# A two-layer hybrid encoder on one core: 32x32 products in half bursts, later diagonal copies, early products in a fixed order

## The chip, the cores and the metric

The kernel runs on one core of a Trainium2 chip. The metric is the device time of one execution in microseconds (us); less is better. The core has a matrix engine (TensorE, PE in the profile, its weight loads PEld), a vector engine (VectorE, DVE), a scalar engine (ScalarE, ACT), GpSimd (POOL) and a sync engine (SyncE, SP) that issues most of the transfers. Each engine runs its own instructions in the order in which they were placed on it, and waits for the others where data or room require it.

## The reference

The reference is an encoder of two layers over 1040 tokens (16 learned ones ahead of 1024) of width 1024, all in 32-bit floating point. Each layer normalises its input, multiplies it by one input matrix, and splits the result. One part feeds a gated delta rule in both directions, 4 heads of 128; the other part is a short gated convolution. Both are joined, multiplied by an output matrix and added to the input. A gated feed-forward block (gate and up, width 2816, then down) follows.

What matters here is the triangular system of the delta rule:

```python
M = jnp.where(strict, jnp.einsum('bnhid,bnhjd->bnhij', kb, k) * decay_mat, 0.0)
A = M + jnp.eye(CHUNK, dtype=M.dtype)
u = lax.linalg.triangular_solve(A, vb, left_side=True, lower=True, unit_diagonal=True)
...
def step(S, inp):
    u_c, w_c, qd_c, kd_c, a_c, gl_c = inp
    v_new = u_c - jnp.einsum('bhcd,bhde->bhce', w_c, S)
    o = jnp.einsum('bhcd,bhde->bhce', qd_c, S) + jnp.einsum('bhij,bhje->bhie', a_c, v_new)
    S = S * gl_c[..., None, None] + jnp.einsum('bhcd,bhce->bhde', kd_c, v_new)
    return S, o
```

The kernel takes chunks of 128 tokens instead of 64, and inverts the 128x128 triangles of all 8 full chunks and 4 heads (32 of them) at once, for each of the two directions.

## The kernel before, in words

**Precision and products.** A 32-bit product is made of three on TensorE: every weight and every input is split into a rounded part (`hi`, copied by ScalarE, line 126) and the rest (`lo`, subtracted by VectorE, line 127), and the matmuls are hi x hi, hi x lo, lo x hi (lines 153, 154, 155). A dense chunk is one call of the inner loop of `dense`: 24 matmuls over 256 to 512 tokens into one bank. Weights come by SyncE's transfers in tiles of 128x512 (`raw`, two buffers), and three buffers each hold their `whi` and `wlo`.

**The order of the work.** A planner places every instruction: it takes the ready instruction of smallest priority number on each engine, by times that it simulates itself, and the engines then run in that order. The code sets priorities: after the first half of a layer the dense matmuls get late ones (`mmp`), so that they fill what other work leaves; `low(f)` places a small product in the same row as the dense ones. Behind each dense chunk `dense` takes one job from each of three lists (`jobs`, `jobs2`, `jobs3`), so that a list of jobs becomes one job a chunk. `after(ins, prev)` adds an edge: `ins` is placed behind `prev`. `wsplit` (line 120) leaves its ScalarE copy in `whi_done[0]`.

**The inverse.** `chunk_p` writes the triangles to `Pv[0]` and `Pv[1]`, one for each direction. `sub_start` (line 524) copies the 32x32 blocks on the diagonal with four ScalarE copies a direction (line 535) and turns them with one VectorE transpose (line 537); the copies of the first direction go to `v[3]`, those of the second to `v[1]` of a scratch tile. `substitute(d)` then inverts all 32x32 blocks by 31 steps of two VectorE instructions (lines 547 and 549). `invert(d)` (line 551) puts the blocks together. It returns jobs: `first` makes 64 products of 32x32 (line 574) and copies them; `second_third` makes 96 (lines 587 and 588), 48 into one bank and 48 into another, each bank with its ScalarE copies (lines 592 and 593) and VectorE copies (lines 594 to 596); five calls of `fourth_fifth` make the 64x64 products (lines 607 and 609). So there are 7 jobs a direction, in `jobs3`: those of the first direction from the last of the four value tiles (line 752), those of the second from the fourth of the eight z and convolution tiles.

**The scan.** `scan_step` (line 815) runs the recurrence chunk by chunk, both directions beside each other. Its scratch `rec` takes the place of the inverse's scratch. The last step of the second direction is the last reader of `Pv[1]` (line 853), whose place the split outputs `oh` and `ol` take (lines 974 and 975). Dense products of the convolution and output projection fill TensorE under the scan.

**The early products.** The feed-forward block uses a scheme with seven half-size products in place of eight. For the first four rows f of the gate and up matrices, the two products of one of its seven (q = 0 and q = 1) are made early, in `early_part(f, q)` (line 1087), beside the end of the output projection: a weight tile is loaded and split (lines 1043 and 1044), then `prod` (line 1056) makes 12 matmuls (lines 1061 to 1063) for each of `NJ` column groups (two of 260 tokens in the first layer, one of 512 in the second), and ScalarE copies the sum out (line 1097). q = 1 adds to the bank that q = 0 filled and that line 1097 has just read. T tiles are prepared meanwhile by `t_split` (lines 1010 and 1011).

Of the kernel before, what the change touches and what calls it, by code (L numbers as in the profile page):

```python
# [42 lines left out]
def trunk(ctx: ExitStack, tc: tile.TileContext, xT, w_in, w_ba, w_out, w_gu, w_dn,  # L43
# [21 lines left out]
    def c4k(tag="c"):  # L65
        return sb.tile([128, L], F32, tag="c", bufs=2, name=nm(tag))
# [47 lines left out]
    mmp = [None]  # L114
    evp = [None]
    jobs, jobs2, jobs3 = [], [], []
    whi_done = [None]
    lov = [False]

    def wsplit(src, hi, lo, raw=None):  # L120

        kk = src.shape[1]
        if raw is None:
            raw = wp.tile([128, WK, 128], F32, tag="raw", bufs=2, name=nm("raw"))
        dma(raw[:, 0:kk, :], src)
        whi_done[0] = act(out=hi, in_=raw[:, 0:kk, :], func=AF.Copy)  # L126
        tt(out=lo, in0=raw[:, 0:kk, :], in1=hi.bitcast(F32), op=ALU.subtract)  # L127

    def wload(src, nk):

# [165 lines left out]
    for l in range(DEPTH):  # L296
# [224 lines left out]
        subs = {}  # L521
        Tm = None

        def sub_start():

            nonlocal Tm
            tmp0.append(big(Y[0][2]))
            Tm = sb.tile([128, 2, 128], F32, tag="off", name=nm("Tm")).rearrange("p a b -> p (a b)")
            v = [tmp0[0][:, i, 0:1024] for i in range(4)]
            for d in range(2):  # L530
                W, Xi = (v[0], v[2]) if d == 0 else [c4k("x")[:, 0:1024] for _ in range(2)]
                W, Xi, dg = (t.rearrange("p (a b) -> p a b", a=32) for t in (W, Xi, v[3 - 2 * d]))
                dma(Xi, eye_d)
                for b in range(4):
                    act(out=dg[B[b]], in_=Pv[d][B[b], :, B[b]], func=AF.Copy)

                nc.vector.transpose(out=W, in_=dg.rearrange("p q i -> p i q"))
                subs[d] = W, Xi

        def substitute(d):  # L540
            W, Xi = subs[d]
# [9 lines left out]
        def invert(d):  # L551
# [15 lines left out]
            def fb(c):  # L567
                return bank("fb"[d]).rearrange("p (q c) -> p q c", c=c)
# [7 lines left out]
                    for (f, s) in pairs:  # L576
                        act(out=QS[B[s], qs, :], in_=ps[B[s]], func=AF.Copy, scale=-1.0)

            def second_third():
                f0, s0 = pairs[0]  # L580
                fo, so = 32 * (f0 % 2), 32 * (s0 % 2)
                for qs in halves:
                    ps = fb(32)

                    def turn(q):
                        for (f, s) in pairs:
                            mm(ps[B[f], q - qs.start, :], QS[B[s], q, :], P_[B[s], q, B[s]], start=True, stop=True, skip_group_check=True)
                        mm(ps[B[s0], q - qs.start, :], P_[B[s0], q, B[s0]], QS[B[s0], q, :], start=True, stop=True, skip_group_check=True)

                    low(lambda: [turn(q) for q in range(qs.start, qs.stop)])  # L590
                    for (f, s) in pairs:
                        act(out=P_[B[f], qs, B[s]], in_=ps[B[f]], func=AF.Copy)
                    act(out=X64[B[s0], qs, fo:fo + 32], in_=ps[B[s0]], func=AF.Copy)
                    nc.vector.tensor_copy(X64[B[f0], qs, fo:fo + 32], XB[B[f0], qs, :])
                    nc.vector.tensor_copy(X64[B[s0], qs, so:so + 32], XB[B[s0], qs, :])
                    nc.vector.memset(X64[B[f0], qs, so:so + 32], 0.0)


            F_, S_ = (slice(0, 64), slice(64, 128)) if d == 0 else (slice(64, 128), slice(0, 64))
# [1 line left out]
            def fourth_fifth(q4, q5):  # L601

                ps = fb(64)

                def turn(q):
                    if q4 is not None:
                        mm(ps[S_, q, :], P_[F_, 8 * q4 + q, S_], X64[F_, 8 * q4 + q, :], start=True, stop=True, skip_group_check=True)
                    if q5 is not None:
                        mm(ps[F_, q, :], X64[S_, 8 * q5 + q, :], P_[S_, 8 * q5 + q, S_], start=True, stop=True, skip_group_check=True)
# [443 lines left out]
        CW = E if E * 4 > 1024 else NB  # L1053
        NJ = NB // CW

        def prod(ps, w, t, j, first, stop=True):
            nk = w[0].shape[1]
            for k in range(nk):
                cs = slice(CW * j, CW * j + CW)
                th, tl = (t[0][k], t[1][k]) if isinstance(t[0], list) else (t[0][:, k, :], t[1][:, k, :])  # L1060
                mm(ps[:, :CW], w[0][:, k, :], th[:, cs], start=first and k == 0, stop=False, skip_group_check=True)  # L1061
                mm(ps[:, :CW], w[0][:, k, :], tl[:, cs], start=False, stop=False, skip_group_check=True)  # L1062
                mm(ps[:, :CW], w[1][:, k, :], th[:, cs], start=False, stop=stop and k == nk - 1, skip_group_check=True)  # L1063

        def raw4(tag):
            if tag == "raw":
# [16 lines left out]

        NE = 4
        early, bks0 = {}, {}

        def early_part(f, q):

            A = raw4("raw")
            dma(A, w_gu[l, f, 0, :, 4 * q:4 * q + 4, :])  # L1090
            w = w_op(A, True)
            if q == 0:
                early[f] = (row(Y[1], F32, 3), row(X[1], F32, 3)) if f < 3 else (row(Y[1] + "f"), c4k())
                bks0[f] = [pbank() for j in range(NJ)]
            for j in range(NJ):
                prod(bks0[f][j], w, T[("B11", "B21")[q]], j, q == 0)
                act(out=part(early[f][1 - q], 0, j), in_=pin(bks0[f][j]), func=AF.Copy)  # L1097

        npar = sb.tile([128, 4], F32, tag="npar", name=nm("npar"))
# [525 lines left out]
```

## Time and profile before

| what | value |
|---|---|
| time, median of 3 runs | 2476.99 us |
| lowest and highest | 2471.99 and 2478.96 us |
| time of the profiled execution | 2479.11 us |
| span of the profiled execution, first to last instruction | 2477.3 us |
| mean granted TensorE clock in it | 0.996 |
| VectorE busy | 1778.2 us, 72% of the span |
| ScalarE busy | 1054.9 us, 43% of the span |

The span is shorter than the time by 1.8 us that lie around it. The profile is one execution, so a sum worked out from its rows stands beside 2479.11 us, not beside the median. Rows of the timeline give start, duration, engine, line, operation, the tile written and the tiles read, size, count, and in brackets how long the engine had been idle and what ended that. Rows by stretches give the busy time of each engine, the granted clock (PEclk; 1.00 is full) and the share of the DMA engines. "issue" as a releaser means that nothing the profile shows ended the wait.

### The profile page before, as it was taken

What the parts mean: (1) busy time and instruction counts of PE and PEld (TensorE: products, weight loads), DVE (VectorE), ACT (ScalarE), POOL (GpSimd) and SP (SyncE); (2) the same over time, 40 slices, a digit from 0 to 9 for tenths busy, and PEclk for the clock granted to TensorE, in tenths of its full rate; (3) what the DMA queues carried; (4) which work ended last, traced back from release to release, by engine and by line L of the source; (5) the groups of instructions that cost most, each with busy time, mean ns of one, the idle gap of its engine ahead of it and who ended that gap; (6) DMA issues with size and microseconds to landing.
All of it is one profiled execution on the core that took longest, in us unless ns stands there. A gap on an engine that the chain in (4) does not pass through costs nothing.

```text
span 2477.3 us, 44868 instructions
## 1 busy us (share of the span) xinstructions
PE 2450.6 (99%) x17530; PEld 2255.6 (91%) x17530; DVE 1778.2 (72%) x3296; ACT 1054.9 (43%) x1964; POOL 67.3 (3%) x157
## 2 busy tenths in 40 slices
PE   9999999999999999999999999999999999999998
PEld 8989999999999999999999888998978888888887
DVE  6888355769877777877657884456798777678774
ACT  6654333445333333444446543334553333334544
POOL 0120000000000000000001100000000000000002
PEclk9999999999999999999999999999999999999999
DMA  4545353534223332674224443445442233238641
GB/s 133 160 146 190 114 166 118 192 93 141 101 94 108 110 102 79 208 238 150 89 83 155 146 159 116 149 138 200 124 139 90 97 107 113 94 106 259 198 138 69
DMA packets 201321, 335.26 MB, mean 135 GB/s; under 512 B 23404, under 2 KB 88356, under 8 KB 201108
## 3 DMA queue, kind: packets, MB, share of 16 engines
q1 hardware_dynamic: 172996, 293.83, 36.9%
q10 hardware_dynamic: 25936, 34.19, 4.3%
q0 software_dynamic: 2176, 4.36, 0.6%
q8 instruction: 138, 2.26, 0.4%
q14 instruction: 75, 0.61, 0.1%
HBM read 250.31 MB, written 81.99 MB: 134 GB/s over the span
## 4 chain that ended last, share of the span: by engine, by line
PE 90%; DVE 4%; DMA 3%; ACT 2%; issue 1%; SPq 0%; ACTq 0%; DVEq 0%
PE pacc L155 10%; PE pacc L153 10%; PE pacc L154 10%; PE pacc L1063 4%; PE pacc L1061 4%; PE pacc L1062 4%; PE pb L1063 3%; PE pb L1061 3%; PE pb L1062 3%; PE pf L1063 3%; PE pf L1061 3%; PE pf L1062 3%; PE pacc L1484 2%; PE pacc L1481 2%; PE pacc L1483 2%; PE pa L1061 1%
## 5 line engine op out<-in xcount | busy, mean ns | idle before, releaser
L153 PE MATMUL pacc<-a,whi 128*128 128x346 f32 (+1 forms) x800 | 262.3, 328 | 1.5 <-ACT whi L126 1.0
L155 PE MATMUL pacc<-a,wlo 128*128 128x346 f32 (+1 forms) x800 | 261.1, 327 | 1.3 <-DVE wlo L127 1.2
L153 PE MATMUL pacc<-b,whi 128*128 128x346 f32 (+2 forms) x672 | 234.5, 349 | 0.6 <-ACT whi L126 0.6
L155 PE MATMUL pacc<-b,wlo 128*128 128x346 f32 (+2 forms) x672 | 233.7, 349 | 0.8 <-DVE wlo L127 0.8
L154 PE MATMUL pacc<-a,whi 128*128 128x346 f32 (+1 forms) x681 | 222.9, 328 | 1.3 <-DVE a L174 0.6
L154 PE MATMUL pacc<-b,whi 128*128 128x346 f32 (+2 forms) x580 | 200.8, 346 | 0.0
L126 ACT ACTIVATE whi<-raw 128x512 fp32r<-128x512 f32 x166 | 104.3, 631 | 218.3 <-PE pacc L154 158.2
L127 DVE TENSOR_TENSOR wlo<-raw,whi 128x512 fp32r<-128x512 f32 x166 | 113.6, 686 | 66.2 <-ACT whi L126 62.6
L155 PEld LDWEIGHTS pacc<-a,wlo 128*128 128x128 f32 x800 | 151.3, 189 | 4.0 <-DVE wlo L127 1.8
L153 PEld LDWEIGHTS pacc<-a,whi 128*128 128x128 f32 x800 | 151.2, 189 | 3.9 <-ACT whi L126 1.2
L153 PEld LDWEIGHTS pacc<-b,whi 128*128 128x128 f32 x672 | 127.2, 189 | 12.2 <-issue 1.9
L155 PEld LDWEIGHTS pacc<-b,wlo 128*128 128x128 f32 x672 | 126.9, 189 | 10.7 <-issue 1.3
L154 PEld LDWEIGHTS pacc<-a,whi 128*128 128x128 f32 x681 | 128.8, 189 | 5.0 <-DVE a L174 1.3
L1043 ACT ACTIVATE whi<-rw 128x512 fp32r<-128x512 f32 x92 | 57.9, 633 | 142.4 <-PE pf L1062 40.8
L154 PEld LDWEIGHTS pacc<-b,whi 128*128 128x128 f32 x580 | 109.8, 189 | 7.0 <-issue 0.4
L1043 ACT ACTIVATE b<-rw 128x512 fp32r<-128x512 f32 x64 | 40.1, 631 | 134.3 <-PE pacc L1062 42.1
L1043 ACT ACTIVATE a<-rw 128x512 fp32r<-128x512 f32 x64 | 40.3, 631 | 93.0 <-PE pacc L1062 60.0
L313 DVE TENSOR_TENSOR a<-pacc,rstd 128x346 f32<-128x346 f32 (+2 forms) x59 | 32.6, 554 | 59.7 <-PE pacc L155 59.4
L1044 DVE TENSOR_TENSOR wlo<-rw,whi 128x512 fp32r<-128x512 f32 x92 | 62.6, 684 | 3.4 <-ACT whi L1043 3.1
L313 DVE TENSOR_TENSOR b<-pacc,rstd 128x346 f32<-128x346 f32 (+1 forms) x63 | 32.2, 513 | 45.2 <-PE pacc L155 45.2
L1061 PE MATMUL pacc<-b,whi 128*128 128x260 f32 (+1 forms) x172 | 53.3, 310 | 0.2 <-ACT c L1097 0.2
L1062 PE MATMUL pacc<-b,whi 128*128 128x260 f32 (+1 forms) x172 | 53.3, 310 | 0.0
(981 smaller groups left out, 7863.6 us busy)
## 6 DMA issues: line engine op xcount, KB each, us to landing
raw<-in_w_in SPq DMA_DIRECT2D x110, 256.0 KB
raw<-in_w_gu SPq DMA_DIRECT2D x104, 256.0 KB
rw<-in_w_gu SPq DMA_DIRECT2D x88, 256.0 KB
rw<-in_w_dn SPq DMA_DIRECT2D x94, 192.0 KB
rec<-vkd SPq DMA_DIRECT2D x61, 256.0 KB
raw<-in_w_out SPq DMA_DIRECT2D x48, 256.0 KB
b<-ad SPq DMA_DIRECT2D x45, 260.0 KB
a<-ad SPq DMA_DIRECT2D x45, 256.0 KB
```

The source lines that it names most:

```text
L126: whi_done[0] = act(out=hi, in_=raw[:, 0:kk, :], func=AF.Copy)
L127: tt(out=lo, in0=raw[:, 0:kk, :], in1=hi.bitcast(F32), op=ALU.subtract)
L153: mm(ps[:, :n], wh, xh[:, n0:n1], start=(k == 0), stop=False)
L154: mm(ps[:, :n], wh, xl[:, n0:n1], start=False, stop=False)
L155: mm(ps[:, :n], wl, xh[:, n0:n1], start=False, stop=(k == K - 1))
L313: tt(out=t[:, n0:n1], in0=ps, in1=rstd[:, n0:n1], op=ALU.mult)
L1043: act(out=hi, in_=src, func=AF.Copy)
L1044: tt(out=lo, in0=src, in1=hi.bitcast(F32), op=ALU.subtract)
L1061: mm(ps[:, :CW], w[0][:, k, :], th[:, cs], start=first and k == 0, stop=False, skip_group_check=True)
L1062: mm(ps[:, :CW], w[0][:, k, :], tl[:, cs], start=False, stop=False, skip_group_check=True)
L1063: mm(ps[:, :CW], w[1][:, k, :], th[:, cs], start=False, stop=stop and k == nk - 1, skip_group_check=True)
L1481: one = mm(ps[:, :CW], wh[:, k, :], th[:, cs], start=st, stop=False, skip_group_check=True)
```

## The change

There are three parts.

1. `second_third` takes one half (16 of the 32 triangles) as its argument and is given to `jobs3` twice. So there are 8 jobs a direction instead of 7, and 48 products of 32x32 follow each other instead of 96.
2. `sub_start` takes the direction. It runs for the first direction at once as before. For the second direction its four copies and its transpose become jobs of `jobs3`, at the 4th, 5th, 7th, 8th and 9th chunk of the value tiles. Each copy is placed behind the weight copy that was issued last (`whi_done[0]`), the transpose behind the last `lo` subtraction (`whi_done[1]`, new).
3. The first matmul of each product of `early_part` is placed behind the last matmul of the product before it, over both column groups, both q and all four f.

```diff
-        whi_done[0] = act(out=hi, in_=raw[:, 0:kk, :], func=AF.Copy)
-        tt(out=lo, in0=raw[:, 0:kk, :], in1=hi.bitcast(F32), op=ALU.subtract)
...
+        whi_done[1] = tt(out=lo, in0=raw[:, 0:kk, :], in1=hi.bitcast(F32), op=ALU.subtract)
...
-            for d in range(2):
-                W, Xi = (v[0], v[2]) if d == 0 else [c4k("x")[:, 0:1024] for _ in range(2)]
...
-                dma(Xi, eye_d)
-                for b in range(4):
-                    act(out=dg[B[b]], in_=Pv[d][B[b], :, B[b]], func=AF.Copy)
-
-                nc.vector.transpose(out=W, in_=dg.rearrange("p q i -> p i q"))
-                subs[d] = W, Xi
+            dma(Xi, eye_d)
+            subs[d] = W, Xi
+            steps = [lambda b=b: after(act(out=dg[B[b]], in_=Pv[d][B[b], :, B[b]], func=AF.Copy), whi_done[0] if d else None) for b in range(4)]
+            return steps + [lambda: after(nc.vector.transpose(out=W, in_=dg.rearrange("p q i -> p i q")), whi_done[1] if d else None)]
...
-            def second_third():
+            def second_third(qs):
...
-                for qs in halves:
-                    ps = fb(32)
...
+                ps = fb(32)
...
-            return [first, second_third] + [lambda a=a, b=b: fourth_fifth(a, b) for a, b in ((0, None), (1, 0), (2, 1), (3, 2), (None, 3))]
+            return [first] + [lambda qs=qs: second_third(qs) for qs in halves] + [lambda a=a, b=b: fourth_fifth(a, b) for a, b in ((0, None), (1, 0), (2, 1), (3, 2), (None, 3))]
...
-        sub_start()
+        for f in sub_start(0):
+            f()
...
+        st1 = sub_start(1)
+        jobs3.extend([None, None, None, st1[0], st1[1], None, st1[2], st1[3], st1[4]])
...
-        def prod(ps, w, t, j, first, stop=True):
+        def prod(ps, w, t, j, first, stop=True, prev=None):
...
-                mm(ps[:, :CW], w[0][:, k, :], th[:, cs], start=first and k == 0, stop=False, skip_group_check=True)
+                one = mm(ps[:, :CW], w[0][:, k, :], th[:, cs], start=first and k == 0, stop=False, skip_group_check=True)
+                if prev is not None and k == 0:
+                    after(one, prev)
...
+                one = mm(ps[:, :CW], w[1][:, k, :], th[:, cs], start=False, stop=stop and k == nk - 1, skip_group_check=True)
+            return one
...
+        turn_e = [None]
...
-                prod(bks0[f][j], w, T[("B11", "B21")[q]], j, q == 0)
+                turn_e[0] = prod(bks0[f][j], w, T[("B11", "B21")[q]], j, q == 0, prev=turn_e[0])
```

More of the change, by code (lines that the diff above doesn't have):

```diff
@@ L116, in trunk @@
     jobs, jobs2, jobs3 = [], [], []
-    whi_done = [None]
+    whi_done = [None, None]
     lov = [False]
@@ L577, in first, with turn @@
                         act(out=QS[B[s], qs, :], in_=ps[B[s]], func=AF.Copy, scale=-1.0)
-            def second_third():
+            def second_third(qs):
                 f0, s0 = pairs[0]
                 fo, so = 32 * (f0 % 2), 32 * (s0 % 2)
-                for qs in halves:
-                    ps = fb(32)
[L585 to L590, printed above, removed]
-                    for (f, s) in pairs:
[L592 to L596, printed above, removed]
+                ps = fb(32)
+                def turn(q):
+                    for (f, s) in pairs:
+                        mm(ps[B[f], q - qs.start, :], QS[B[s], q, :], P_[B[s], q, B[s]], start=True, stop=True, skip_group_check=True)
+                    mm(ps[B[s0], q - qs.start, :], P_[B[s0], q, B[s0]], QS[B[s0], q, :], start=True, stop=True, skip_group_check=True)
+                low(lambda: [turn(q) for q in range(qs.start, qs.stop)])
+                for (f, s) in pairs:
+                    act(out=P_[B[f], qs, B[s]], in_=ps[B[f]], func=AF.Copy)
+                act(out=X64[B[s0], qs, fo:fo + 32], in_=ps[B[s0]], func=AF.Copy)
+                nc.vector.tensor_copy(X64[B[f0], qs, fo:fo + 32], XB[B[f0], qs, :])
+                nc.vector.tensor_copy(X64[B[s0], qs, so:so + 32], XB[B[s0], qs, :])
+                nc.vector.memset(X64[B[f0], qs, so:so + 32], 0.0)
             F_, S_ = (slice(0, 64), slice(64, 128)) if d == 0 else (slice(64, 128), slice(0, 64))
```

11 lines of the change are left out of this document (6 added, 5 removed).

## The prediction

> **What bounds the kernel now.** I read the page first, then the waits of TensorE, then the timeline around the longest of them, then the stretches for the clock.
>
> ```profile
> span 2477.3 us, 44868 instructions
> ...
> PE 2450.6 (99%) x17530; PEld 2255.6 (91%) x17530; DVE 1778.2 (72%) x3296; ACT 1054.9 (43%) x1964; POOL 67.3 (3%) x157
> ...
> q8 instruction: 138, 2.26, 0.4%
> ```
>
> TensorE is the bound: its 99% leaves 27 us in which it does nothing. No part of the change removes a product, so it can only win from such gaps and from time at a lower clock. The waits of TensorE, longest in total first (engine, what waited, what for: us, times, longest):
>
> ```profile
> PE pf L587 <- issue: 2.5, 2, 2.1
> PE pb L1061 <- ACT whi L1043: 2.0, 1, 2.0
> ...
> PE pb L587 <- issue: 1.9, 1, 1.9
> ```
>
> Line 587 belongs to `second_third` and 1061 to the early products; the waits for weight splits, part 2, are of the same size and follow with their rows.
>
> **Part 1, half bursts.** One call of `second_third` appears in the rows of its two lines, then the burst in the second layer's first and second direction and in the first layer's first direction:
>
> ```profile
> L587 PE MATMUL pf<-P,a x128: 191/191/256, 1448.6 to 1452.9; 32*32 32x32 f32 x128
> ...
> L588 PE MATMUL pf<-a,P x64: 191/191/256, 1448.6 to 1452.9; 32*32 32x32 f32 x64
> ```
> ```profile
> 1450.46 0.19 PE L588 MATMUL pf<-a,P 32*32 32x32 f32 x1
> 1452.72 0.26 PE L587 MATMUL pf<-P,a 32*32 32x32 f32 x2 [2.07 <-issue]
> ...
> 1523.09 0.21 PE L587 MATMUL pb<-P,a 32*32 32x32 f32 x2 [1.89 <-issue]
> ...
> 208.37 0.22 PE L587 MATMUL pf<-P,b 32*32 32x32 f32 x2 [0.40 <-issue]
> ```
>
> A call is 128 + 64 = 192 matmul records and as many weight loads, 384 instructions. From 1448.6 to 1450.46 they pass at about 5 ns each (12 records of the 192 come after the stall), then TensorE stands with nothing to wait for. The page's instruction queue says what is missing: 2.26 MB over 2 x 17530 instructions is 64 bytes each, and 2.26 MB over 138 packets is 16.4 KB, or some 256 instructions a packet. Narrowed to 1450.2 to 1451.2, the view of the queues shows one such packet, and none from 1443.5 to 1450.2:
>
> ```profile
> q8 instruction: 1, 0.02, 5.5%
> ```
>
> TensorE goes on about 2.5 us after that packet starts, so the instructions ran out. Over the whole span an instruction takes 2477 / 35060 = 71 ns, so 256 last 18 us. In the burst they last 256 x 5 ns = 1.3 us. A half has 192 instructions and takes 1 us; a chunk of 48 lies between the halves, and it takes about 4 us (a chunk and one later job take 5.08 us in the rows of the scan term). So any 256 last 1 + 4 = 5 us, twice the 2.5 us. I take the stalls as gone: 2.07 + 1.89 + 0.40 us idle, and 0.19 us each for the last product ahead of it, under which the next ones would have started, **4.9 us**. The fourth call, at 272.8, has no such row, so a stall depends on where the packets' borders fall. `first` stays as it is, and has no such wait in its four calls.
>
> Each long stall was followed by a stretch at half clock (its row: length, busy time of PE, PEld, DVE, ACT and POOL, granted clock, DMA share, GB/s):
>
> ```profile
> 1452.74:1456.15 3.41, 3.41 (x22) 2.86 (x23) 1.85 (x5) 2.36 (x4) 0.00 (x0) 0.50 0.02 5
> 1524.42:1527.83 3.41, 3.41 (x9) 2.63 (x8) 0.00 (x0) 0.88 (x2) 0.00 (x0) 0.50 0.00 0
> 1821.38:1824.79 3.41, 3.41 (x9) 2.62 (x9) 3.41 (x6) 1.46 (x3) 0.00 (x0) 0.50 0.27 76
> ...
> 152.26:155.67 3.41, 2.02 (x11) 1.73 (x12) 3.36 (x5) 2.21 (x4) 3.14 (x7) 1.00 0.14 37
> ```
>
> TensorE is busy throughout, so 3.41 us at 0.50 lose 1.7 us. Two of the three belong to the bursts: **3.4 us**. (The last row shows that 1.4 us idle in such a stretch did not bring the next one down.) Part 1: 8.3 us.
>
> The Trainium skill, "Runtime: NRT & Kernel Launch", section "Instruction fetch mechanics", gives TensorE room for 2048 instructions, refilled in blocks of 256. By that rule a burst of 384 would not run dry, part 1 would bring nothing, and the time would be that of the third rival below; the packet that lands inside the stall speaks against it.
>
> **Part 2, diagonal copies.** ScalarE, VectorE and TensorE in the first layer, then the second layer:
>
> ```profile
> L535 ACT ACTIVATE b<-P x8: 1041/1056/1062, 143.2 to 150.7; 32x1024 f32<-32x1024 f32 x8
> ...
> 151.79 1.15 ACT L126 ACTIVATE whi<-raw 128x512 fp32r<-128x512 f32 x2
> ...
> 169.42 0.63 ACT L126 ACTIVATE whi<-raw 128x512 fp32r<-128x512 f32 x1 [1.58 <-PE pacc L154]
> ```
> ```profile
> 147.50 2.08 DVE L537 STREAM_TRANSPOSE b<-b 128x1024 f32<-128x1024 f32 x1 [2.18 <-ACT b L535]
> ```
> ```profile
> 152.47 0.42 PE L153 MATMUL pacc<-a,whi 128*128 128x348 f32 x1 [0.99 <-ACT whi L126]
> ...
> 154.87 0.42 PE L155 MATMUL pacc<-a,wlo 128*128 128x348 f32 x1 [1.19 <-DVE wlo L127]
> ...
> 1393.27 0.43 PE L153 MATMUL pacc<-b,whi 128*128 128x348 f32 x1 [0.65 <-ACT whi L126]
> ...
> 1395.70 0.43 PE L155 MATMUL pacc<-b,wlo 128*128 128x348 f32 x1 [0.77 <-DVE wlo L127]
> ```
>
> The weight copies for the first value tile stand behind eight diagonal copies on ScalarE. With four of them gone they start 4 x 1.06 = 4.2 us earlier, at 147.5, and end at 148.7, ahead of TensorE's need at 151.5. The `lo` parts are late next: VectorE is free of the first transpose at 149.6 and gives them at 150.3 and 150.9, still in time. So all four waits go: 0.99 + 1.19 + 0.65 + 0.77 = 3.6 us, and 0.1 us more for each matmul that starts cold (0.42 for 0.32): **4.0 us**. Left over would be at most the `lo` waits, 2.0 us.
>
> The four copies (4.3 us) and the transpose (2.0 us) come back later, behind weight copies of the second and third value tile. What queues behind them on ScalarE is the silu and convolution of the value tiles and the next weight copy. That one waits for TensorE to free its buffer (1.58 us idle at 169.42, with a whole tile of three chunks, 12 us, still to run before it is needed), so they cost nothing; without that cover two copies in a row would cost 2.1 us each time. The transposed blocks are needed by the second substitution, whose first instruction runs at 198.3:
>
> ```profile
> L547 DVE TENSOR_TENSOR Tm<-x,x x62: 180/360/425, 198.3 to 1487.1; 128x31 f32<-128x31 f32 x4, 128x60 f32<-128x60 f32 x4, 128x87 f32<-128x87 f32 x4, 128x112 f32<-128x112 f32 x4
> ```
>
> Even the ninth chunk ends ahead of that (152.5 + 9 x 4 = 188.5). The scratch `v[1]` is written again only in the second half of `second_third`, some 20 us later. The transfer of the unit blocks is issued on SyncE's queue a little later, for the same use.
>
> **Part 3, early products.** TensorE and ScalarE in the first layer's and second layer's early products:
>
> ```profile
> 588.72 0.39 PE L1061 MATMUL pf<-b,whi 128*128 128x260 f32 x1 [0.45 <-ACT whi L1043]
> ...
> 592.79 0.39 PE L1063 MATMUL pf<-b,wlo 128*128 128x260 f32 x1 [0.68 <-DVE wlo L1044]
> ...
> 603.23 0.39 PE L1061 MATMUL pa<-a,whi 128*128 128x260 f32 x1 [0.77 <-ACT c L1097]
> ```
> ```profile
> 1818.23 0.39 PE L1063 MATMUL pacc<-a,wlo 128*128 128x512 f32 x1
> 1820.65 0.50 PE L1061 MATMUL pb<-a,whi 128*128 128x512 f32 x1 [2.03 <-ACT whi L1043]
> ...
> 1821.21 0.52 PE L1061 MATMUL pacc<-b,whi 128*128 128x512 f32 x1
> ```
> ```profile
> 1820.50 0.58 ACT L1097 ACTIVATE b<-pacc 128x512 f32<-128x512 f32 x1
> ```
>
> At 1820.65 two matmuls of row f = 2 (bank `pb`) stand ahead of f = 1, q = 1 (`pacc<-b`), and wait for their weights. In order, `pacc<-b` would be first. But it adds to a bank that line 1097 reads until 1821.08, so it could not start before 1821.2 in any order: the wait stays, and the two matmuls that were done meanwhile come later (0.5 us). In the first layer two column groups hide that read, and the order saves perhaps what it costs. Where the next `lo` parts are late, VectorE is full (3.41 of 3.41 us in the third half-clock row), and the order does not speed it up. Bounds: all four waits and one half-clock stretch go, -5.6 us; or the two first matmuls of each product lose their cover, 7 borders x 0.47 in the second layer and 15 x 0.24 in the first, +6.9 us. I take **0**, by the last row, and count the edge itself (same engine, same order) as free.
>
> **What the extra job costs.** The second direction's last job comes one chunk later, and the scan starts behind it. Two of these jobs, then the scan's last step of the second layer (its last input on ScalarE, its products on TensorE):
>
> ```profile
> 1547.77 0.27 PE L607 MATMUL pb<-a,P 64*64 64x64 f32 x1
> ...
> 1552.85 1.14 PE L609 MATMUL pb<-P,a 64*64 64x64 f32 x16
> ...
> 1760.88 1.05 PE L853 MATMUL pb<-vv,P 128*128 128x128 f32 x8
> ...
> 1762.24 0.28 PE L153 MATMUL pacc<-o,whi 128*128 128x256 f32 x1
> ```
> ```profile
> 1755.29 1.15 ACT L850 ACTIVATE qs<-pb,negE 128x128 f32<-128x128 f32 x4 [1.16 <-PE pb L848]
> ```
>
> So the scan starts 5.08 us later against the dense work. Its last products run at 1760.88, though their last input was there at 1756.44: 4.44 us of slack. The output products, which need the room that those products free, begin at once behind them. 5.08 - 4.44 leaves **0.6 us**; nothing at best, 5.1 us if the planner keeps its distances. In the first layer the last output is split at 521.6 and first used at 532.9, so 5.08 us there cost nothing:
>
> ```profile
> 520.13 1.44 DVE L975 TENSOR_TENSOR o<-b,o 128x260 fp32r<-128x260 f32 x4
> ```
> ```profile
> 532.89 0.28 PE L153 MATMUL pf<-o,whi 128*128 128x260 f32 x1
> ```
>
> **Sum.** 2479.1 - 8.3 - 4.0 + 0 + 0.6 = 2467.4 us, from the profiled execution; that one lies 2.1 us above the median of the runs shown, so the gain against the median is 9.6 us, 0.39%. A measurement of this kernel tells about 0.3%, 7.4 us, from no change: 2469.6 is the border.
>
> **Rivals.** (a) The order also wins the waits of part 3: 2467.4 - 5.6 = 2461.8 us. For it: four such rows; against: the read of the bank at 1820.50. (b) The scan's delay is all seen: 2467.4 + 4.5 = 2471.9 us. For it: output products right behind line 853; against: 4.44 us of slack. (c) The stall belongs to these products, whatever the burst's length, so part 1 does nothing: 2479.1 - 4.0 + 0.6 = 2475.7 us. Against it: the call at 272.8 without a stall. (d) Slower: the fixed order takes TensorE's cover at each of the second layer's 7 borders between early products, and each shows the gap of 1818.23 to 1821.21 (2.6 us beyond a matmul), with three more half-clock stretches: 7 x 2.6 - 2.0 + 3 x 1.7 = 21.3, so 2488.7 us. It decides the sign from (11.7 + 2.0) / 7 = 2.0 us a border. For it: line 1097 must be passed every second border, and the planner filled those gaps with later products; against: at the other borders no bank is shared.
>
> **Chances.** Forecast 0.55 (2463 to 2472 by itself, about three quarters of that below 2469.6: 0.41 faster, 0.14 same); (a) 0.10, faster; (b) 0.10, same; (c) 0.07, same; (d) 0.14, slower; 0.04 for a shuffled plan that eats the gain, same. Together faster 0.51, same 0.35, slower 0.14. The range 2460 to 2478 takes in all but (d) and little else.
>
> **What would show it.** Part 1 is right if lines 587 and 588 run in eight stretches of about 1 us with no "issue" wait, and no half clock follows them. Part 2 is right if line 153 has no wait behind the first direction's copies, and wrong if a weight copy elsewhere is now late behind line 535. Part 3 is as I say if the wait at `pacc<-b` in the second layer remains, released by line 1097. The scan term is seen in TensorE's idle time ahead of the first `o` product of the second layer. The prediction fails if new waits on lines 1061 or 153 add up to several us.

## The result, and the profile after

| | median, us | lowest to highest | runs |
|---|---|---|---|
| before | 2477.09 | 2471.99 to 2479.76 | 22 |
| after | 2471.79 | 2467.43 to 2479.62 | 22 |

The ratio of after to before is 0.9985, with a 95% interval from 0.9978 to 0.9991: 0.15%, or 3.7 us by the ratio and 5.3 by the medians. The forecast was 9.6 us. So the change is faster, but by 40 to 55% of what was forecast, and by less than the 0.3% that the prediction took as the least that a measurement tells; with 22 runs on each side 0.15% could be told.

The profiled execution of after happens to be one of its slowest, 2478.96 us. Its total tells nothing beside the 2479.11 of before; what can be compared is stall by stall. First the page, then TensorE's longest waits (what waited, what for: us, times, longest):

```profile
span 2477.2 us, 44855 instructions
...
PE 2451.8 (99%) x17530; PEld 2259.3 (91%) x17530; DVE 1778.8 (72%) x3296; ACT 1053.9 (43%) x1964; POOL 67.3 (3%) x157
```
```profile
PE pb L474 <- DVE P L483: 2.5, 2, 1.8
PE pacc L1061 <- ACT b L1101: 2.1, 1, 2.1
PE pf L584 <- issue: 2.0, 1, 2.0
PE pf L604 <- ACT b L590: 2.0, 2, 1.7
```

Lines have moved: 584 and 585 were 587 and 588, 589 and 590 were 592 and 593, 604 and 606 were 607 and 609, 1064 and 1065 were 1062 and 1063, 1101 was 1097, 545 and 547 were 547 and 549. The waits for `whi` and `wlo` at lines 153 and 155 have left the list, and so has the stall of `pb` (the second direction). But one stall of `pf` (the first direction) is there as before, the early products wait as long as before for another releaser, and two lines are new: 604 and 474. The last stems from VectorE waiting for a transfer (`ptm<-gd`); in the twelve profiles below it is 0.2 to 1.4 us, so I leave it out.

**Part 1.** The first row is the second layer's first direction, the second row its second direction. Behind the colon stand the shortest, median and longest product in ns, and then the times of the first and last start:

```profile
L584 PE MATMUL pf<-P,a x128: 191/191/254, 1450.7 to 1455.1; 32*32 32x32 f32 x128
...
L584 PE MATMUL pb<-P,a x128: 191/191/212, 1519.5 to 1527.4; 32*32 32x32 f32 x128
```

In the second direction the 128 records are spread over 7.9 us, because a dense chunk lies between the halves. In the first direction they are not. The timeline of TensorE there, with the first and last product ahead of the stall and the first behind it:

```profile
1450.74 0.22 PE L584 MATMUL pf<-P,a 32*32 32x32 f32 x2
...
1452.58 0.19 PE L585 MATMUL pf<-a,P 32*32 32x32 f32 x1
1454.82 0.26 PE L584 MATMUL pf<-P,a 32*32 32x32 f32 x2 [2.04 <-issue]
```

There is no other instruction between the halves: 174 products run, then TensorE stands for 2.04 us, then the last 18 run. **The two half bursts are one burst again.** So they are in the first layer's first direction (starts from 208.9 to 211.2), but that one has no stall. In place of the eight stretches that the prediction named as its sign there are six. Between 1452.3 and 1452.6 the view of the queues shows one packet of instructions, as in the stall before, and TensorE goes on 2.2 to 2.5 us after it:

```profile
q8 instruction: 1, 0.02, 22.2%
```

The stretches say the same of the clock (length, busy time of PE, PEld, DVE, ACT and POOL, PEclk, DMA share, GB/s):

```profile
218.41:221.82 3.41, 3.41 (x13) 3.41 (x13) 2.83 (x6) 2.15 (x4) 0.00 (x0) 0.50 0.59 163
...
1454.03:1460.86 6.83, 6.04 (x40) 5.98 (x40) 5.43 (x13) 3.36 (x6) 0.00 (x0) 0.50 0.93 324
...
1519.30:1528.00 8.70, 8.70 (x220) 7.01 (x219) 2.73 (x4) 3.77 (x6) 0.00 (x0) 1.00 0.32 119
```

The parted call (last row) keeps TensorE busy for all of its 8.70 us at full clock. The call in one piece is followed by 6.83 us of half clock, two stretches of 3.41. The first row belongs to the new wait at line 604.

**Part 2.** Between 148 and 160 us both waits of before are gone; TensorE has one other wait there, and it is not for a weight:

```profile
PE pa L731 <- ACT b L756: 0.6, 1, 0.6
```

In the second layer, between 1386 and 1400 us, there is none. So the four waits have gone as forecast. But the first direction's substitution, which VectorE makes meanwhile, has moved. Its second instruction before, then after:

```profile
L549 DVE TENSOR_TENSOR b<-b,Tm x31: 193/355/426, 149.9 to 194.0; 128x31 f32<-128x31 f32 x2, 128x60 f32<-128x60 f32 x2, 128x87 f32<-128x87 f32 x2, 128x112 f32<-128x112 f32 x2
```
```profile
L547 DVE TENSOR_TENSOR b<-b,Tm x31: 189/359/428, 152.1 to 198.2; 128x31 f32<-128x31 f32 x2, 128x60 f32<-128x60 f32 x2, 128x87 f32<-128x87 f32 x2, 128x112 f32<-128x112 f32 x2
```

It ends 4.2 us later. Times of two executions can differ by that much without the change (in e3 below, which has no part 2, this row ends at 198.5), but its place in the order has moved too: 921 dense matmuls have started before its last instruction in each of the five profiles without part 2, and 948 to 958 in each of the nine with it. The first direction's products come later with it, and their copies meet something that stood behind them before. ScalarE, then TensorE, in the first layer of after (ACTq is an issue of a transfer on ScalarE's queue):

```profile
212.78 0.33 ACTq L512 DMA_DIRECT2D dt<-dtd  x1
213.16 1.19 ACT L589 ACTIVATE P<-pf 32x512 f32<-32x512 f32 x2 [2.33 <-DVE Tm L545]
214.36 0.59 ACT L590 ACTIVATE b<-pf 32x512 f32<-32x512 f32 x1
215.66 0.33 ACTq L512 DMA_DIRECT2D dt<-dtd  x1
216.04 1.19 ACT L589 ACTIVATE P<-pf 32x512 f32<-32x512 f32 x2 [1.09 <-DVE x L547]
217.23 0.59 ACT L590 ACTIVATE b<-pf 32x512 f32<-32x512 f32 x1
```
```profile
215.00 1.14 PE L604 MATMUL pf<-b,P 64*64 64x64 f32 x16 [0.22 <-ACT b L590]
217.88 0.32 PE L604 MATMUL pf<-b,P 64*64 64x64 f32 x2 [1.74 <-ACT b L590]
```

The burst's last products start at 211.2, and its copies could start then. They start at 213.16 and 216.04, each behind the issue of a load into a decay tile. TensorE loses 0.22 + 1.74 us, and the clock 1.7 us more behind it.

**Part 3.** The two waits of the first layer at 588.72 and 592.79 are gone, the one for line 1101 is still there. In the second layer the wait at `pacc<-b` is as long as before; TensorE, then ScalarE:

```profile
1818.62 0.50 PE L1061 MATMUL pacc<-b,whi 128*128 128x512 f32 x1 [2.12 <-ACT b L1101]
```
```profile
1816.51 0.63 ACT L1043 ACTIVATE whi<-raw 128x512 fp32r<-128x512 f32 x1 [1.81 <-DMA raw<-in_w_gu]
1817.05 1.04 ACT L1010 ACTIVATE P<-b 128x1024 fp32r<-128x1024 f32 x1
1817.99 0.58 ACT L1101 ACTIVATE b<-pacc 128x512 f32<-128x512 f32 x1
```

The bank is full at about 1816.5, but the copy that reads it stands on ScalarE behind a weight copy and a split. The weight copy has waited for its transfer, but starts just as the bank is full; so the 1.5 us until 1817.99 are the run time of these two, and the read itself takes 0.58 us.

### The profile page after: what moved, and what is told of

Read it like the earlier page. It is cut to its first block, busy times and chain, and to the rows that moved or that the text cites. A ratio compares the mean times of both kernels' runs of the same rounds, so it can differ in the third digit from the quotient of the medians.

```text
span 2477.2 us, 44855 instructions
## 1 busy us (share of the span) xinstructions
PE 2451.8 (99%) x17530; PEld 2259.3 (91%) x17530; DVE 1778.8 (72%) x3296; ACT 1053.9 (43%) x1964; POOL 67.3 (3%) x157
## 4 chain that ended last, share of the span: by engine, by line
PE 89%; DVE 5%; DMA 3%; ACT 2%; issue 1%; SPq 0%; ACTq 0%; DVEq 0%; POOLq 0%
PE pacc L153 10%; PE pacc L154 10%; PE pacc L155 10%; PE pacc L1065 4%; PE pacc L1061 4%; PE pacc L1064 4%; PE pb L1061 3%; PE pb L1064 3%; PE pb L1065 3%; PE pf L1065 3%; PE pf L1061 3%; PE pf L1064 3%; PE pacc L1488 2%; PE pacc L1485 2%; PE pacc L1487 2%; PE pa L1061 1%
## 5 line engine op out<-in xcount | busy, mean ns | idle before, releaser
L1061 PE MATMUL pacc<-b,whi 128*128 128x260 f32 (+1 forms) x172 | 53.3, 310 | 2.1 <-ACT b L1101 2.1
L1065 PE MATMUL pacc<-b,wlo 128*128 128x260 f32 (+1 forms) x172 | 53.3, 310 | 0.0
```

The lines of the kernel that those rows point to most:

```text
L1061: one = mm(ps[:, :CW], w[0][:, k, :], th[:, cs], start=first and k == 0, stop=False, skip_group_check=True)
L1065: one = mm(ps[:, :CW], w[1][:, k, :], th[:, cs], start=False, stop=stop and k == nk - 1, skip_group_check=True)
```

## The experiments

They were run in four groups on three chips, each group beside the kernel before, so kernels of different groups are compared by their ratio to it. The theory: of three parts each does what its rows show, part 1 only where a dense chunk really parts the halves, part 2 less the new wait on ScalarE's queue, part 3 nothing. The rival: the forecast's sum was right, and something else in the kernel takes it back. The line that gives out the inverse's jobs, and the line that calls the early parts, are those that most edits touch.

### Each part alone

**e1**, with `sub_start` and `prod` as before:

```diff
+            return [first] + [lambda qs=qs: second_third(qs) for qs in halves] + [...]
```


> Part 1 alone. In the trace of the changed kernel only the second directions have a dense chunk between the halves; in the first directions the 96 products still follow each other (174 records from 1450.74 to 1452.58, 2.2 us idle, 18 more), so the name of half bursts holds in two of four calls. Theory: only the stall of the second layer's second direction goes, 1.89 idle + 0.19 + 1.7 of half clock = 3.8 us, less 0.6 for the later scan: 3.2 us faster than before, about 2473.9 us, and the first direction of the second layer still shows an idle time of about 2 us in its 32x32 products. Rival A, the prediction as put: all three stalls go, 7.7 us faster, 2469.4. Rival B: the packets' borders only move, 2477.

Measured: 2474.49 us, ratio 0.9992 (0.9984 to 1.0001). The rows of TensorE in the second layer, and its largest wait for "issue":

```profile
L584 PE MATMUL pf<-P,a x128: 191/191/254, 1447.5 to 1451.5; 32*32 32x32 f32 x128
L584 PE MATMUL pb<-P,a x128: 191/191/212, 1517.3 to 1525.2; 32*32 32x32 f32 x128
```
```profile
PE pf L585 <- issue: 1.8, 1, 1.8
```

In the second layer one direction is parted and runs through, the other is not and stalls; the first layer's first direction, in one piece too, stalls for 0.7 us. The time agrees with the theory (2 us by the ratio, 3.2 expected) and excludes the 7.7 us of rival A; rival B, no change, just touches the interval, but the stall of `pb` is gone from the trace.

**e2**, with `second_third` in one job and `prod` as before:

```diff
+        st1 = sub_start(1)
+        jobs3.extend([None, None, None, st1[0], st1[1], None, st1[2], st1[3], st1[4]])
```


> Part 2 alone. Theory: the four waits for weight parts go (4.0 us), but the first direction's inverse comes 3 us later in the first layer, and the fourth and fifth products there then wait for copies that stand on ScalarE behind transfer issues: about 2 us idle at 214 to 218 (1.74 us in the changed kernel) and often 1.7 us of half clock. Sum 0.3 to 2.0 us faster than before, 2475 to 2477 us. Rival, that this new wait comes from part 1: no such wait here, 4.0 us faster, 2473.1.

Measured: 2475.99 us, ratio 0.9996 (0.9985 to 1.0006), as the theory had it: 1 us by the ratio, which is not clear of no change; the rival's 4.0 us (0.9984) lie just outside. The new wait comes with part 2 alone:

```profile
217.55 0.32 PE L604 MATMUL pf<-b,P 64*64 64x64 f32 x2 [1.26 <-ACT b L590]
```

**e3**, with `second_third` in one job and `sub_start` as before:

```diff
+                turn_e[0] = prod(bks0[f][j], w, T[("B11", "B21")[q]], j, q == 0, prev=turn_e[0])
```


> Part 3 alone. Theory, as predicted: no change, 2477.1 us, with the wait of about 2 us in the second layer at pacc now ended by the copy that reads its bank. Rival A: the order wins its waits, 5.6 us faster, 2471.5. Rival B: the order takes away the cover of each product's first matmuls, up to 6.9 us slower, 2484.

Measured: 2477.84 us, ratio 1.0012 (1.0003 to 1.0021): 3 us slower, which none of the three had as its number, though it lies between no change and rival B. The trace shows both waits of the first layer gone (1.13 us), the one in the second layer longer, 2.4 us instead of 2.0, and a new one there of 0.5 us for line 1100 (1101 in after); together they leave about nothing. So the 3 us are not accounted for by the waits. The mean granted clock is 0.9955 over the 11 runs and 0.9962 over the 29 of before beside them; by my estimate that is 1.7 us of the 3. Why the clock was lower is not shown.

### The first directions really parted

**e4**, all three parts, and empty places in the first direction's list:

```diff
-            return [first] + [lambda qs=qs: second_third(qs) for qs in halves] + [...]
+            return ([first, None, None, None, None, None, lambda: second_third(halves[0]), None, None, lambda: second_third(halves[1])] if d == 0 else ...) + [...]
```


> The changed kernel, with empty places put into the first direction's list of jobs (five between first and the first half, two between the halves), so that 36 dense matmuls lie between the halves in the first layer and 72 in the second; the second direction as in the changed kernel. Theory: the stall in the second layer's first direction (2.2 us) goes with its stretches of half clock (6.83 us at 0.5 in the profile, 3.4 us), and the wait of the fourth and fifth products in the first layer (1.74 us and 1.7 us of half clock) as well: 4 to 9 us faster than the changed kernel, 2463 to 2468 us. Rival: the stall is not the row of instructions but the packet's place: another burst stalls instead, or the later first direction costs as much, 2471.8.

Measured: 2468.12 us (2466.18 to 2469.22), ratio 0.9968 (0.9955 to 0.9980): 0.17% less than after, 4.2 us, which the two intervals leave 3.5 us either way. Expected were 4 to 9. The first direction's products in the first and second layer, and the stretch of the second layer's:

```profile
L584 PE MATMUL pf<-P,b x128: 191/191/212, 208.5 to 218.8; 32*32 32x32 f32 x128
...
L584 PE MATMUL pf<-P,a x128: 191/191/212, 1444.5 to 1462.8; 32*32 32x32 f32 x128
```
```profile
1444.50:1462.80 18.30, 17.73 (x293) 17.26 (x295) 16.40 (x39) 4.75 (x8) 0.00 (x0) 1.00 0.90 305
```

The stall has gone, and with it the wait at line 604 in the first layer: between 205 and 222 us TensorE waits for nothing. In this execution no stretch is at half clock from the start-up to the last 12 us.

**e7**, as e4, but with both halves in one job again, in both directions:

```diff
-            return ([first, None, None, None, None, None, lambda: second_third(halves[0]), None, None, lambda: second_third(halves[1])] if d == 0 else ...) + [...]
+            return ([first, None, None, None, None, None, (lambda: [second_third(qs) for qs in halves])] if d == 0 else [first, lambda: [second_third(qs) for qs in halves]]) + [...]
```


> The kernel with parted halves, with both halves in one job again in both directions, the empty places and parts 2 and 3 kept: all four calls are rows of 96 products. Theory: the stalls of the second layer come back in both directions (about 2.2 and 1.8 us idle), the wait of the first layer's fourth and fifth products as well (1.3 to 2 us), and each brings half a stretch at half clock or one, 0.9 to 1.7 us: 7 to 10 us slower than with parted halves, 2475 to 2478 us. Rival: the empty places alone made the difference, 2468.

Measured: 2476.13 us, ratio 0.9997 (0.9985 to 1.0009): 0.29% or 7.2 us slower than e4, as expected, and 7.3 us slower by the medians than e6 below, which is parted too and ran beside it. Three of its four calls stall; the first layer's first direction, then both of the second layer:

```profile
212.71 0.21 PE L585 MATMUL pf<-b,P 32*32 32x32 f32 x1 [1.18 <-issue]
```
```profile
1452.82 0.18 PE L585 MATMUL pf<-a,P 32*32 32x32 f32 x1 [1.31 <-issue]
```
```profile
1519.80 0.26 PE L584 MATMUL pb<-P,a 32*32 32x32 f32 x1 [2.16 <-issue]
```

The empty places alone bring nothing; the parted burst does. One detail missed: the wait at line 604 did not come back, and the 1.18 us in the first layer were not expected. The two trade with each other: the stall and the wait at 604 in the first layer are 0 and 1.96 us in after, 0.4 and 1.3 in e2, 0.9 and 0 in e5, 1.2 and 0 here. As I read it, products that a stall has made late no longer wait for the late copies. Which call stalls, and for how long, moves with the place where the packets end.

### Part 2 with the other stalls away, and ScalarE's queue

**e10**, as e8 below, but without part 2 (`sub_start` for both directions at once):

```diff
-        for f in sub_start(0):
-            f()
+        for d in range(2):
+            for f in sub_start(d):
+                f()
...
-        st1 = sub_start(1)
-        jobs3.extend([None, None, None, st1[0], st1[1], None, st1[2], st1[3], st1[4]])
```


> The parted kernel with alternated early parts, without part 2 (diagonal copies of both directions at once, as before). Theory: the four waits for weight parts come back, 3.6 + 0.4 us as predicted, nothing else: 4.0 us slower than with part 2 (2466.3), 2470.3 us. Rival: part 2 is worth only what it was measured alone, 1 us, since the later first direction takes the rest back by more than the one wait seen: 2467.3.

Measured: 2472.17 us, ratio 0.9976 (0.9967 to 0.9985) beside 0.9957 with part 2: 0.19%, 4.7 us, and the two intervals leave about 3.5 us either way. The waits are back, between 148 and 160 us and (second fence) between 1380 and 1400:

```profile
PE pacc L155 <- DVE wlo L127: 1.2, 1, 1.2
PE pacc L153 <- ACT whi L126: 1.0, 1, 1.0
```
```profile
PE pacc L155 <- DVE wlo L127: 0.8, 1, 0.8
PE pacc L153 <- ACT whi L126: 0.7, 1, 0.7
```

The four waits are 3.7 us. The two kernels ran in different groups, so the profiles decide: TensorE stands for 23.3 us in that of e10 and 18.3 in that of e8 (span less busy time), at about the same mean clock over all runs (0.9981 and 0.9982). The predicted waits are there where the later first direction hits nothing; the time, 4.7 with 3.5 either way, agrees.

**e9**, all three parts, with the decay tiles' loads issued by GpSimd:

```diff
-                adma(dt_[0:n, :, 0:n], dtd[c, d]...)
+                qdma(dt_[0:n, :, 0:n], dtd[c, d]...)
```


> The changed kernel, with the loads of the decay tiles (line 512) issued by GpSimd instead of ScalarE. In the first layer of the changed kernel ScalarE's copies of the 32x32 products stand right behind such an issue, idle 2.33 and 1.09 us, and the fourth and fifth products wait 1.74 us for them. Theory: the issue holds up ScalarE until its tile is free; with it on another queue the wait at about 217 us goes, with it half a stretch at half clock: 1.7 to 3.4 us faster than the changed kernel (2471.8), 2468.4 to 2470.1 us; the stall in the second layer's first direction stays. Rival: the copies wait for VectorE, which the trace names, busy with the substitution: the wait stays, 2471.8.

Measured: 2474.78 us, ratio 0.9986 (0.9978 to 0.9995), the same as after (0.9985). The wait itself behaved as the theory said. ScalarE in the first layer:

```profile
214.23 1.17 ACT L589 ACTIVATE P<-pf 32x512 f32<-32x512 f32 x2
215.41 0.59 ACT L590 ACTIVATE b<-pf 32x512 f32<-32x512 f32 x1
216.03 1.19 ACT L589 ACTIVATE P<-pf 32x512 f32<-32x512 f32 x2
```

The copies follow each other with no idle time, and TensorE does not wait at line 604. So it was the issue that held them and not the VectorE instruction that the row named; VectorE runs the same substitution here. But the 1.7 to 3.4 us did not appear in the time. The profile shows a part of what they went into: a wait of 1.2 us at line 445 for ScalarE's copy (line 447), which after does not list, and one of 2.0 us in the first 15 us, where after has 0.3. The second I take for this execution's transfer; the first comes again in e11. The rest stays open.

### The order of the early products

**e5**, parts 1 and 2 only, and **e6**, as e4 without part 3:

```diff
-                turn_e[0] = prod(..., prev=turn_e[0])
+                turn_e[0] = prod(...)
```


> The changed kernel without part 3 (parts 1 and 2). The order alone was measured 3.0 us slower than before (0.7 to 5.2). Theory: it costs as much beside the other parts, so this kernel is 0.7 to 5 us faster than the changed one (2471.8), about 2469.5 us. Rival: the order's two waits in the first layer (0.45 and 0.68 us) come back and nothing else changes, 1 us slower than the changed kernel, 2473.

> The kernel with all halves parted, without part 3. Same question where no burst stalls: theory, 0.7 to 5 us faster than with the order (2468.1), about 2466 us; rival, the order saves 1 us or nothing, 2468 to 2469.

Measured: e5 2472.33 us, ratio 0.9981 (0.9972 to 0.9989), beside 0.9985 with the order; e6 2468.86 us, ratio 0.9966 (0.9955 to 0.9977), beside 0.9968. Beside the other parts neither a gain nor a loss by the order is seen, within 0.11% for e5 and 0.17% for e6. So of the theory's 0.7 to 5 us the part up to 3.6 us (e5) or 4.6 us (e6) stays possible; the measured differences are 1.0 and 0.5 us.

**e8**, as e4, and **e12**, part 3 alone, both with another order of the last five early parts:

```diff
-        for f, q in ((1, 1), (2, 0), (2, 1), (3, 0), (3, 1)):
+        for f, q in ((2, 0), (1, 1), (3, 0), (2, 1), (3, 1)):
```


> The kernel with parted halves, with the last five early parts given out in another order, (2,0) (1,1) (3,0) (2,1) (3,1) instead of (1,1) (2,0) (2,1) (3,0) (3,1), still each behind the one before: a whole product lies between the filling of a bank and the next product that adds to it. Theory: the wait of 2.28 us in the second layer, ended by the copy that reads the bank, goes, and with it a stretch at half clock in some runs: 2.3 to 4 us faster than the parted kernel (2468.1), 2464 to 2466 us. Rival: the wait is for weights as well (the weight copies stand there behind transfers), and the row in front of (1,1) waits as long, 2468.

Measured: 2466.26 us (2465.73 to 2469.27), ratio 0.9957 (0.9946 to 0.9968): 0.11% or 2.7 us below e4, as expected, but the two intervals overlap, so the time alone does not show it. TensorE's waits between 1795 and 1832 us, which in e4 were headed by the 2.1 us for line 1101:

```profile
PE pa L1061 <- ACT b L1043: 1.0, 1, 1.0
PE pacc L1065 <- DVE wlo L1044: 0.5, 1, 0.5
PE pb L1065 <- DVE wlo L1044: 0.4, 1, 0.4
```

The wait at the bank is gone; some of its time comes back as weights that are late. By the ratio this is the fastest kernel of the study, 0.43% below before and 0.28% below after.

> Part 3 alone, with the last five early parts alternated, (2,0) (1,1) (3,0) (2,1) (3,1). The order alone was 0.12% slower than before (0.03 to 0.21), though its waits in the first layer were fewer. Theory: what it lost lies at the second layer's bank, where it waited 2.4 us (2.6 between the starts beyond the usual) instead of 2.0, and in the half clock behind that; alternated, the wait goes: ratio 0.998 to 0.999 of before, about 2473 to 2475 us. Rival: the loss lies in the edges elsewhere, or was chance of the half-clock stretches: the alternation gives the 2.4 us back and the ratio stays between 1.000 and 1.001.

Measured: 2475.93 us, ratio 0.9999 (0.9987 to 1.0011), 0.13% below e3 and thus about the wait's size, though with 0.15% either way it is not clear of no change; and it should have been 0.998 to 0.999 if the bank were all. Some 2 us of the order alone stay unexplained, or are chance.

**e11**, as e8, with the edit of e9:

```diff
-                adma(dt_[0:n, :, 0:n], dtd[c, d]...)
+                qdma(dt_[0:n, :, 0:n], dtd[c, d]...)
```


> The parted kernel with alternated early parts and the decay tiles' loads on GpSimd. That kernel has no wait of the fourth and fifth products left, so theory: no change against 2466.3 us (within 1 us). Rival: ScalarE's other copies get free of the issues too (the scan's and the value tiles'), 2 us faster, 2464.

Measured: 2471.69 us, ratio 0.9973 (0.9964 to 0.9982): 0.16%, 4 us slower than e8, where no change or 2 us faster was expected. The profiles show where: TensorE stands for 21.6 us in that of e11 and for 18.3 in that of e8 (span less busy time), 1.4 us of the difference at line 445 (1.7 us for line 447 instead of 0.3), and ahead of the last 12 us there are two stretches of half clock in place of one, 1.7 us. Together that is 5.0 of the 5.2 us between the two profiled executions. Line 445 waits for 1.2 and 1.7 us in the two profiles with this edit and for at most 1.0 in the twelve others; why its copies come later is not shown. So moving the issues off ScalarE has no general gain.

## Why the prediction was right in part

- **Part 1, the stalls: the step that failed.** The prediction said that "a chunk of 48 lies between the halves". That holds for the order in which the code gives out jobs, not for the order in which the planner places instructions. In the second directions it held, and the second layer's stall there (2.08 us with its cold product) went. In the first directions the dense chunk ran ahead of both halves and none lay between them; the rows above and e1 show it, e4 repairs it, e7 undoes the repair. That the first half came late because of its copies from `first` is my reading and not shown. About half of the 4.9 us were not delivered: 2.04 us of idle stayed in the second layer's first direction. The 0.40 us in the first layer's first direction went by luck, for that burst is not parted either, and in e1 it stalls for 0.7.
- **Part 1, the cause.** That the instructions run out, and that 256 of them must not pass faster than a packet comes, was right: none of the 28 parted calls in the fourteen profiles stalls, and 21 of the 28 in one piece do (the other seven are all in the first layer). In each of the 21 stalls TensorE goes on 2.3 to 2.7 us after a packet of instructions starts. The packet again lands inside the stall, so the Trainium skill's "Runtime: NRT & Kernel Launch", section "Instruction fetch mechanics", by which 384 instructions would find room, is again not what the traces show.
- **Part 1, the clock: mis-sized.** I counted one stretch of 1.7 us for each stall, as in the one profile. It differs from execution to execution (last section), so 3.4 us were too much even for two stalls that go, and only one of them went. I also left out the fourth stretch of that profile, at 510.66 us, which follows no stall.
- **Part 2, the waits.** The rows that go and, in e10, come back are 3.6 and 3.7 us; with the cold starts that is the 4.0 of the sum, and e10's time (4.7) agrees. **Part 2, "they cost nothing": failed.** I asked what queues behind the moved copies, and not what moves with them: the first direction's substitution came later (by 4.2 us, and by some 30 dense matmuls in the order), its products' copies met the decay tiles' loads on ScalarE, and 1.96 us of idle time and a stretch of half clock came back in the profile of after. e9 shows that the issue held the copies. Alone, the part was worth 1 us.
- **Part 3: 0** agrees with e5 and e6, and the wait stayed with line 1101 as its releaser, as the prediction said it would. But its reason was incomplete: it is not only the read of the bank, 0.58 us, but the place of the copy on ScalarE, 1.5 us behind a weight copy and a split; and "in any order" was wrong, since e8 removes the wait by another order.
- **The scan: 0.6** has the right size in the trace, but at another place. The output products of the second layer follow the last products of line 853 directly, as before, and TensorE waits for nothing there; from 1560 to 1800 us it has 0.61 us ahead of line 853 at 1701.08 and 0.17 just behind, where before has no wait. Rival (b) gave the time that came out, 2471.9, by chance: its mechanism, 5.1 us of delay, did not occur.
- **Rivals (a), (c) and (d).** Of (a) two of four waits went, 0.45 and 0.68 us, but not the one of 2 us. (c) is excluded by the parted calls. (d) did not occur: the gap stands at one border only.

By the rows, then: part 2's 3.6 us, 1.89 and 0.40 us of stalls and 1.13 us of part 3's waits went, and 1.96 us at line 604 and some 2 us of small waits (lines 731, 853, 1061 and 1065) came. That leaves about 3 us, and what the half clock takes in the mean run: its granted clock is 0.9965 over the 22 runs of after and 0.9959 over the 96 of before in the experiments' groups, by my estimate 1.5 us. 3.7 to 5.3 us were measured. The time lies within the prediction's range, but that range is 18 us wide and takes in no change as well, so it says little for the sum.

## What to carry to other kernels

Parting a job into two changes nothing unless something is placed between the parts: look in the trace (first and last start of the line) whether it is there, and make the gap by a due time or an edge where a planner can slide work past. Where a copy is moved off the critical path, follow what else shifts with it to the next place at which engines queue; a transfer issue in an in-order engine's queue is such a place. Where a bank is filled twice, put another product between the fillings.

## What the runs showed of the hardware

The half clock comes in stretches of 3.41 us or twice that, and whether a stall is followed by one is not set by its length alone. In e12 both directions of the second layer stall for about 2 us. Stretches around each (columns as above):

```profile
1448.10:1451.51 3.41, 1.81 (x19) 1.59 (x20) 3.13 (x9) 1.98 (x4) 0.00 (x0) 1.00 0.15 48
1451.51:1454.92 3.41, 3.41 (x29) 2.81 (x28) 1.99 (x5) 1.75 (x4) 0.00 (x0) 1.00 0.26 77
1516.40:1519.81 3.41, 1.47 (x45) 1.19 (x35) 0.75 (x1) 2.62 (x6) 0.00 (x0) 1.00 0.64 234
1519.81:1523.22 3.41, 3.41 (x10) 2.67 (x9) 0.00 (x0) 1.00 (x2) 0.00 (x0) 0.50 0.00 1
```

With 1.60 us idle in its stretch the first is followed by full clock; with 1.94 us the second is followed by 0.50. All starts of half clock in one execution lie a whole number of 3.413 us apart (before: 1452.74 and 1524.42 are 21 such steps), so a stall that falls across a border of that grid is divided. Nor is a stall needed. This is the fourth stretch of before and the step ahead of it:

```profile
507.24:510.66 3.42, 3.42 (x26) 2.42 (x26) 1.77 (x3) 0.00 (x0) 0.00 (x0) 1.00 0.31 85
510.66:514.07 3.41, 3.41 (x14) 3.41 (x13) 1.13 (x5) 1.81 (x9) 0.00 (x0) 0.50 0.02 1
```

TensorE is busy throughout, about 2 us of the first row with 16x16 products (lines 874 and 876), and half clock follows; it does at this place in five of the fourteen profiles. In after, a step with 1.81 us idle (from 1375.53) is followed by full clock, and the stall of the second layer, divided into 1.26 and 0.79 us among 32x32 products, by two stretches of half clock. So idle time alone does not set the clock; what else does is not shown here. The Trainium skill's "TensorE: Matmul & The Clock Gate", section "Why this matters for your kernels", advises against idle gaps above about 3 us; here 2 us were enough. The half clock also explains much of the spread: the fastest run of after (2467.43 us) had a mean granted clock of 0.998, the slowest (2479.62) 0.994, and 0.004 of 2470 us are 9.9 us of the 12.2 between them. A kernel without long stalls should be steadier as well. The few runs of e4 (five, 2466.18 to 2469.22), e6 (six, 2468.09 to 2470.18) and e8 (six, 2465.73 to 2469.27) look so; the eleven each of e10 (2469.01 to 2475.79) and e11 (2469.42 to 2474.14) spread less than those of most kernels with stalls, but not less than the twelve of e5 (2470.14 to 2475.85).
